# Closing a token mixer one head at a time, and a router constant from one matrix product

## The chip, the cores and the metric

The kernel runs on one core of one Trainium2 chip. The metric is the device time of one execution in microseconds (us); lower is better. The core has five engines that run their own queues in order and meet through semaphores: PE (TensorE, matrix products and transposes, with weight loads PEld), DVE (VectorE), ACT (ScalarE), POOL (GpSimd) and SP, which here only issues DMAs. A small share of the DMAs is issued from ACT's queue.

## The reference

A float32 model of two parts, 512 tokens by 1024 features. Two blocks (feed-forward, hybrid mixer, feed-forward) come first. Then a third block: a modulated token mixer (`token_mixer`) and an expert-choice mixture of experts (MoE), and a last norm. What the change touches is the end of the token mixer and the router:

```python
# token mixer, end: o is [1, 512, 4 heads, 128]
o = rmsnorm(o, dn_norm) * silu(gate)          # norm over 128 features of a head, one weight row for all heads
y = concatenate([o.reshape(B, L, 512), pooled], -1) @ w_out     # [512, 1024] @ [1024, 1024]
x = x + g1 * y
# mixture of experts
h = rmsnorm(x, norm2) * (1 + scale2) + shift2
aff = softmax(h @ w_router)                   # w_router: [1024, 16]
top_aff, top_idx = top_k(aff.T, 64)           # each expert takes 64 tokens
```

Each of 16 experts then applies a gated feed-forward (three 1024x1024 matrices) to its 64 tokens.

## The kernel before

Activations lie feature-major: `g.x[k]` is the k-th block of 128 features (partitions) by 512 tokens. A product in nearly full float32 precision is made of three passes (`mm3`, L69 to L71): weights and activations are split into a rounded part and a remainder (`whi`, `wlo`; `xh`, `xl`), one cast on ACT and one subtraction on DVE (`split`, L39 and L40). `load_w` loads a weight block into one of two `wraw` buffers and splits it into `whi`/`wlo`, of which there are three buffers each. The program is written in one order; a scheduler that runs when the program is built fixes the order of each engine's queue, and it may bring an instruction forward of where it is written.

The end of `token_mixer`. A recurrence over chunks (gated delta rule) writes `o_acc[c]` (in the profile `t_raw`), four tiles of 128 tokens by 512, four heads side by side. While it still runs, PE projects the gates (`gate`, in the profile `t_b`: ACT and DVE make their silu, L1403 to L1405) and begins the output product: `begun[t]`, t = 0 to 3, are four PSUM accumulators of 128 output features by 512 tokens, in which the pooled half of the input (blocks 4 to 7) has been summed. Then, when the recurrence is over:

- `oss` and `rsqrt` give `orn`, 1/rms for each token and head;
- for each of the four token tiles c, DVE scales the four heads by `orn` and by the norm weights `rows` (L1432, 16 instructions of 128x128), and POOL multiplies the tile by the gate (L1434, 4 of 128x512);
- PE transposes 128x128 blocks (L1438), four for a head k, into one PSUM bank, and `split` makes `yh[:, k]`, `yl[:, k]` of it (`xh`, `xl` in the profile). All four tiles c are needed for any head k.

`mixer_out` then finishes `begun[t]` with blocks 0 to 3 (12 matmuls of 512 columns for each t) from a weight block loaded by `load_w`, adds each to `g.x[t]` (`add`, L1452), and makes t = 4 to 7 with 24 matmuls each.

`mixer_out` is a generator: `moe` runs a step of its own for each block k that comes out: a square for the norm (ACT, POOL), `logits(k-1)` (L1557: 8 PE instructions, `r_ww` by x) and `turn_x(k-1)` (L1563: 4 transposes). The router weights `wr` (`r_w`) are loaded when `moe` begins, from ACT's queue (L1544), into a tile of the `moe` pool, whose memory overlaps that of the token mixer's tiles. `wrw` (`r_ww`) is `wr` times the norm weight (POOL, L1548). At k = 1 the constant `cst`, the shift times the router weights, is made by eight accumulated products of a broadcast column of `shift` with `wr` (L1576). After the last block come the router's softmax and the choice of 64 tokens for each expert (`route`), the gathering of the first two experts' tokens, and the experts, whose weights SP loads in chunks of 1 MB (L1534, L1539), 17 chunks ahead.

Of the kernel before, what the change touches and what calls it, by code (L numbers as in the profile page):

```python
# [11 lines left out]
F32 = mybir.dt.float32  # L12
# [9 lines left out]
NK = D // 128  # L22
# [14 lines left out]
def split(g, hi, lo, src):  # L37

    g.nc.scalar.copy(hi, src)  # L39
    g.nc.vector.tensor_sub(lo, src, f32(hi))  # L40
# [91 lines left out]
def stat_tiles(g):  # L132

    t = g.xpool.tile([128, 2 * S], F32, name="x")
    return t[:, :S], t[:, S:]
# [62 lines left out]
def bc(ap, shape):  # L198
    return ap.to_broadcast(shape)
# [52 lines left out]
def fm_proj(g, xh, xl, w, c0=0, ks=range(NK), k0=0, pump=None, p=None, last=True):  # L252


    first = p is None
    if first:
        p = g.ps_m.tile([128, 512], F32, name="mm")
    wh, wl = w
    cs = slice(c0, c0 + 128)
    mm3(g, p, lambda k: (wh[:, k - k0, cs], wl[:, k - k0, cs]), lambda k: (xh[:, k, :], xl[:, k, :]), ks, pump, first, last)  # L260
    return p
# [24 lines left out]
def sm(g):  # L286
    return g.ps_s.tile([128, 512], F32, name="sm")
# [963 lines left out]
def token_mixer(g, I):  # L1251
# [148 lines left out]
    for i, p in enumerate(ps):  # L1400
        z = gate[i // 2][:, i % 2, :]
        th = ring()
        nc.scalar.activation(th, p, AF.Tanh, scale=0.5)  # L1403
        nc.scalar.activation(z, p, AF.Copy, scale=0.5)
        nc.vector.scalar_tensor_tensor(z, th, 1.0, z, op0=OP.add, op1=OP.mult)  # L1405
        side.pump(4)
    pooled(3)

# [17 lines left out]
    nc.vector.scalar_tensor_tensor(oss, oss, 1.0 / 128, qe, op0=OP.mult, op1=OP.add)  # L1426
    orn = P.tile([128, NT, 4], F32, name="t_orn")
    rsqrt(g, orn, oss, P, "to")
    for c in range(NT):
        for h in range(4):  # L1430
            hs = slice(h * 128, (h + 1) * 128)
            nc.vector.scalar_tensor_tensor(o_acc[c][:, hs], o_acc[c][:, hs], orn[:, c, h:h + 1], rows,  # L1432
                                           op0=OP.mult, op1=OP.mult)
        nc.gpsimd.tensor_mul(o_acc[c], o_acc[c], gate[c // 2][:, c % 2, :])  # L1434
    for k in range(4):
        p = sm(g)
        for i in range(NT):
            nc.tensor.transpose(p[:, i * 128:(i + 1) * 128], o_acc[i][:, k * 128:(k + 1) * 128], g.ident)  # L1438
        split(g, yh[:, k, :], yl[:, k, :], p)
    return yh, yl, xd, begun  # L1440


def mixer_out(g, I, yh, yl, xd, begun):

    nc = g.nc
    order = (4, 5, 6, 7, 0, 1, 2, 3)
    g.xt = x_tiles(g)
    g.x = x_views(g.xt)
    for c in range(4):
        nc.sync.dma_start(g.xt[c].rearrange("p (k t) -> p k t", k=2), xd[2 * c:2 * c + 2].rearrange("k p t -> p k t"))  # L1450
    def add(t, p):
        nc.vector.scalar_tensor_tensor(g.x[t], p, g.mod[:, 16 + t:17 + t], g.x[t], op0=OP.mult, op1=OP.add)  # L1452

    w = load_w(g, I["w_out2"][0:512, 0:512], 512, 256)
    for t, p in enumerate(begun):
        add(t, fm_proj(g, yh, yl, w[t // 2], (t % 2) * 128, (0, 1, 2, 3), 0, p=p))
        yield t
    for c in range(2, 4):
        w = load_w(g, I["w_out2"][:, c * 256:(c + 1) * 256], 256)
        for m in range(2):  # L1460
            t = 2 * c + m
            add(t, fm_proj(g, yh, yl, w[m], 0, order))
            yield t
# [39 lines left out]
def moe(g, I, P, x_out, out):  # L1503
# [36 lines left out]
            loaded.append(raw)  # L1540


    wr = P.tile([128, NK, 16], F32, name="r_w")
    nc.scalar.dma_start(wr, I["w_router"].rearrange("(k p) e -> p k e", p=128))  # L1544
    wrw = P.tile([128, NK, 16], F32, name="r_ww")
    w = P.tile([128, NK], F32, name="nm_w")
    nc.vector.scalar_tensor_tensor(w, g.mod[:, 32:40], 1.0, v["norm2"], op0=OP.add, op1=OP.mult)
    nc.gpsimd.tensor_mul(wrw, wr, bc(w[:, :, None], [128, NK, 16]))  # L1548
    cst = P.tile([128, 16], F32, name="r_cst")
    acc, sq = stat_tiles(g)  # L1550
    pr = sm(g)

# [13 lines left out]
    for k in x_out:  # L1566
        nc.scalar.activation(sq if k else acc, g.x[k], AF.Square)
        if 0 < k < NK - 1:
            nc.gpsimd.tensor_add(acc, acc, sq)
        if k:  # L1570
            logits(k - 1)
            turn_x(k - 1)
        if k == 1:
            ps = sm(g)
            for j in range(NK):
                nc.tensor.matmul(ps[:, 0:16], bc(shift[:, j:j + 1], [128, 128]), wr[:, j, :], start=(j == 0),  # L1576
                                 stop=(j == NK - 1))
            nc.scalar.copy(cst, ps[:, 0:16])
        if k in (1, 3, 5):
            while len(loaded) < NR * (k + 1) // 6:  # L1580
                load()
# [308 lines left out]
def setup(g, I, P0):  # L1890
    nc = g.nc
    C = g.const
    _, at, _ = constants()
    cst = C.tile(list(I["cst"].shape), F32, name="cst")
    nc.scalar.dma_start(cst, I["cst"])
    for n, sl in at[0].items():
        setattr(g, n, cst[:, sl])

    r = g.small.tile([128, 284], F32R, name="cstr")
    for src, c0, c1 in ((g.ident, 0, 128), (g.mneg, 128, 256), (g.stk, 256, 284)):  # L1900
        nc.scalar.copy(r[:, c0:c1], src)
    g.eye_r, g.neg_r, g.stk8, g.stk4 = [r[:, a:b] for a, b in ((0, 128), (128, 256), (272, 280), (280, 284))]
    sel = g.small.tile([128, 16, 32], F32R, name="sel16")
    nc.scalar.copy(sel, bc(g.stk[:, 0:16][:, :, None], [128, 16, 32]))
    g.sel16 = sel.rearrange("p (t h) c -> p t (h c)", t=4)
    vecf = C.tile(list(I["vecf"].shape), F32, name="vecf")
    nc.scalar.dma_start(vecf, I["vecf"])
    g.vecr = I["vecr"]
    pf = [0]

    def tf(k):
        pf[0] += k
        return vecf[:, pf[0] - k:pf[0]]

    g.V = []
    for L in range(2):
        v = {}
        v["ffn1_norm"], v["mix_norm"], v["ffn2_norm"] = tf(8), tf(8), tf(8)
        v["conv_w"], v["conv_b"] = tf(32), tf(8)
        v["qk_w"] = tf(2)  # L1920
        v["snorm"] = tf(4)
        nc.vector.tensor_scalar(v["conv_w"], v["conv_w"], 0.5, None, op0=OP.mult)
        nc.vector.tensor_scalar(v["conv_b"], v["conv_b"], 0.5, None, op0=OP.mult)
        nc.vector.tensor_scalar(v["qk_w"][:, 0:1], v["qk_w"][:, 0:1], 32.0 ** -0.5, None, op0=OP.mult)
        g.V.append(v)
    v = dict(norm1=tf(8), norm2=tf(8), b_mod=tf(48), conv_w=tf(48), pool_scale=tf(4), c=tf(16), norm_f=tf(8))
    nc.vector.tensor_scalar(v["conv_w"], v["conv_w"], 0.5, None, op0=OP.mult)
    r2 = C.tile([128, 16], F32, name="row2")
    nc.scalar.dma_start(r2, bass.AP(tensor=I["vecr2"].tensor, offset=I["vecr2"].offset, ap=[[0, 128], [1, 16]]))
    v["dt_bias"], v["negA"] = r2[:, 0:8], r2[:, 8:16]  # L1930
    nc.scalar.activation(v["negA"], v["negA"], AF.Exp)
    nc.vector.tensor_scalar(v["negA"], v["negA"], -1.0, None, op0=OP.mult)
    g.V2 = v
    g.mod = C.tile([128, 48], F32, name="mod")
    g.modc = C.tile([128, 16], F32, name="modc")


def spread(g, I):
# [120 lines left out]
```

## Time and profile before

| | |
|---|---|
| median of 3 runs | 3046.94 us (3042.88 to 3048.18) |
| the profiled execution's own time | 3047.01 us |
| its span, first to last instruction | 3045.0 us |
| mean granted TensorE clock, as a share of 2.4 GHz | 0.971 |
| busy: PE, DVE, ACT, POOL | 95%, 54%, 30%, 10% of the span |
| DMA traffic | 471.51 MB, mean 155 GB/s |

Times in the profile are us from the span's start. A row of the timeline is a run of like instructions on one engine: start, duration, engine, source line, operation, output<-input, shape, count, and in brackets the idle time before it with what ended that. "x8" counts instructions as the profiler saw them; a 128x128 float32 product with 16 columns shows as two instructions. A matmul's duration includes the pipeline, so the rate is read from one start to the next.

### The profile page before, as it was taken

How to read it: one execution, taken by the hardware profiler on the slowest of the kernel's cores; microseconds unless marked ns; L12 is line 12 of the kernel's file. 1: busy time of each engine (PE TensorE's matmuls, PEld its weight loads, DVE VectorE, ACT ScalarE, POOL GpSimd, SP SyncE). 2: the span in 40 equal slices, each digit the busy share in tenths (PEclk: the TensorE clock that was granted, in tenths of full speed). 3: DMA queues.
4: the chain of work that ended last, by engine and by line, in shares of the span. 5: the costliest groups of instructions: out<-in, count | busy, mean ns of one | idle time of the engine just before them, and what ended most of it. 6: DMA issues, size and time to landing. Idle time of an engine off the chain costs nothing. (4 is left out here: it accounts for less than half of the span.)

```text
span 3045.0 us, 37744 instructions
## 1 busy us (share of the span) xinstructions
PE 2895.9 (95%) x15232; PEld 2220.4 (73%) x15232; DVE 1648.2 (54%) x2839; ACT 910.2 (30%) x1523; POOL 313.4 (10%) x260
## 2 busy tenths in 40 slices
PE   7999998999999999999899999999998877999998
PEld 6888886878888888888787788888787765444445
DVE  4445457665444599545586666554765643122213
ACT  3222335443222332223454433222342321010002
POOL 0001003110101102011130201201100010000000
PEclk9999999999999999999999999999999988999998
DMA  4433343122332358333421333222323435999996
GB/s 144 128 97 97 102 143 120 53 87 83 97 97 93 115 195 299 100 93 132 142 63 59 103 101 111 86 76 90 114 71 90 116 150 201 397 423 424 423 423 253
DMA packets 293107, 471.51 MB, mean 155 GB/s; under 512 B 45215, under 2 KB 237727, under 8 KB 269508
## 3 DMA queue, kind: packets, MB, share of 16 engines
q1 hardware_dynamic: 290216, 466.28, 43.5%
q10 hardware_dynamic: 2716, 2.82, 0.3%
q8 instruction: 120, 1.97, 0.3%
q14 instruction: 55, 0.45, 0.0%
HBM read 449.38 MB, written 19.67 MB: 154 GB/s over the span
## 5 line engine op out<-in xcount | busy, mean ns | idle before, releaser
L69 PE MATMUL mm<-xh,whi 128*128 128x512 f32 x1952 | 780.0, 401 | 15.6 <-ACT xh L146 8.4
L70 PE MATMUL mm<-xl,whi 128*128 128x512 f32 x1952 | 774.2, 397 | 0.0
L71 PE MATMUL mm<-xh,wlo 128*128 128x512 f32 x1952 | 770.6, 395 | 1.1 <-DVE wlo L40 1.1
L39 ACT CAST whi<-wraw 128x1024 fp32r<-128x1024 f32 (+3 forms) x390 | 391.7, 1005 | 1123.3 <-PE mm L70 795.0
L40 DVE TENSOR_TENSOR wlo<-wraw,whi 128x1024 fp32r<-128x1024 f32 (+3 forms) x390 | 516.6, 1325 | 106.5 <-ACT whi L39 99.2
L69 PEld LDWEIGHTS mm<-xh,whi 128*128 128x128 f32 x1952 | 372.9, 191 | 99.5 <-ACT xh L146 9.3
L71 PEld LDWEIGHTS mm<-xh,wlo 128*128 128x128 f32 x1952 | 372.0, 191 | 79.4 <-DVE wlo L40 1.9
L70 PEld LDWEIGHTS mm<-xl,whi 128*128 128x128 f32 x1952 | 372.5, 191 | 76.2 <-DVE xl L147 1.2
L69 PE MATMUL mm<-hh,whi 128*128 128x512 f32 x704 | 279.3, 397 | 0.0
L70 PE MATMUL mm<-hl,whi 128*128 128x512 f32 x704 | 278.6, 396 | 0.0
L71 PE MATMUL mm<-hh,wlo 128*128 128x512 f32 x704 | 278.3, 395 | 0.0
L192 POOL TENSOR_TENSOR x<-x,dt 128x512 f32<-128x512 f32 x72 | 112.9, 1568 | 873.2 <-DVE dt L191 778.6
L172 DVE TENSOR_TENSOR gs<-mm,rb 128x512 f32<-128x512 f32 x88 | 60.8, 691 | 202.9 <-PE mm L71 198.5
L177 DVE TENSOR_TENSOR gs<-gs,mm 128x512 f32<-128x512 f32 x88 | 60.4, 687 | 197.1 <-PE mm L71 197.0
L191 DVE SCALAR_TENSOR_TENSOR dt<-mm,rb 128x512 f32<-128x512 f32 x104 | 71.8, 690 | 166.9 <-PE mm L71 166.9
L71 PEld LDWEIGHTS mm<-hh,wlo 128*128 128x128 f32 x704 | 132.1, 188 | 32.1
L70 PEld LDWEIGHTS mm<-hl,whi 128*128 128x128 f32 x704 | 132.2, 188 | 31.7 <-DVE hl L40 0.3
L69 PEld LDWEIGHTS mm<-hh,whi 128*128 128x128 f32 x704 | 132.1, 188 | 31.6
L1651 PE MATMUL mm<-e_raw,e_x 128*64 128x512 f32 x504 | 118.9, 598 | 0.0
L238 PE MATMUL mm<-whi,xh 128*128 128x512 f32 (+2 forms) x288 | 103.3, 359 | 0.0
L240 PE MATMUL mm<-whi,xl 128*128 128x512 f32 (+2 forms) x288 | 100.0, 348 | 0.0
L239 PE MATMUL mm<-wlo,xh 128*128 128x512 f32 (+2 forms) x288 | 99.7, 346 | 0.0
(649 smaller groups left out, 3555.4 us busy)
## 6 DMA issues: line engine op xcount, KB each, us to landing
wraw<-ffn_gate SPq DMA_DIRECT2D x44, 1024.0 KB, 5.4
wraw<-ffn_up SPq DMA_DIRECT2D x44, 1024.0 KB, 5.3
wraw<-w_in SPq DMA_DIRECT2D x38, 1024.0 KB, 5.3
e_raw<-e_gate SPq DMA_DIRECT2D x36, 1024.0 KB, 12.4
e_raw<-e_up SPq DMA_DIRECT2D x27, 1024.0 KB, 13.2
e_raw<-e_down SPq DMA_DIRECT2D x25, 1024.0 KB, 13.2
wraw<-ffn_down SPq DMA_DIRECT2D x24, 1024.0 KB, 5.1
mw<-w_mod SPq DMA_DIRECT2D x24, 1024.0 KB, 5.1
```

The lines of the kernel that those rows point to most:

```text
L39: g.nc.scalar.copy(hi, src)
L40: g.nc.vector.tensor_sub(lo, src, f32(hi))
L69: g.nc.tensor.matmul(out, lh, rh, start=first and i == 0, stop=False, skip_group_check=not (first and last))
L70: g.nc.tensor.matmul(out, lh, rl, start=False, stop=False, skip_group_check=not (first and last))
L71: g.nc.tensor.matmul(out, ll, rh, start=False, stop=last and i == n - 1, skip_group_check=not (first and last))
L172: nc.vector.tensor_mul(gs, pg, rb)
L191: nc.vector.scalar_tensor_tensor(t, pd, 0.25, rb, op0=OP.mult, op1=OP.mult)
L192: (nc.vector if c0 + nch == sum(groups) else nc.gpsimd).tensor_add(g.x[2 * c + m], g.x[2 * c + m], t)
L238: nc.tensor.matmul(o, xh[:, kk, ts], wh[:, k, :], start=(kk == 0), stop=False)
L239: nc.tensor.matmul(o, xh[:, kk, ts], wl[:, k, :], start=False, stop=False)
L240: nc.tensor.matmul(o, xl[:, kk, ts], wh[:, k, :], start=False, stop=(kk == NK - 1))
L1651: nc.tensor.matmul(ps[h][pj[j], :], lhs(k, j), raw[j][:, h * 512:(h + 1) * 512], start=(k == 0), stop=(k == NK - 1), skip_group_check=True)
```

## The change

Four edits. (1) The norm weights are multiplied into the gates as each gate tile is made (POOL, new line under L1405, 4 instructions of 128x512), and POOL's multiplication of `o_acc` by the gate goes away: DVE's 16 instructions now multiply by `orn` and by the gate. (2) The 16 are ordered by head: four for head k, its transposes and split, then the 12 matmuls that head k contributes to the four `begun` tiles; the weights for these are loaded in `token_mixer` instead of in `mixer_out`, which only adds the finished tiles. (3) The router weights go into a tile of the constants' pool and are loaded in `setup`, at the beginning of the kernel. (4) The constant: POOL multiplies the router weights by the shift into `ws` (128 x 16 x 8), DVE sums over 8, and one product with a matrix of ones sums over the partitions, in place of eight products.

```diff
@@ token_mixer
         nc.vector.scalar_tensor_tensor(z, th, 1.0, z, op0=OP.add, op1=OP.mult)
+        nc.gpsimd.tensor_mul(hv(z), hv(z), bc(rows[:, None, :], [128, 4, 128]))
         side.pump(4)
...
     rsqrt(g, orn, oss, P, "to")
-    for c in range(NT):
-        for h in range(4):
-            hs = slice(h * 128, (h + 1) * 128)
-            nc.vector.scalar_tensor_tensor(o_acc[c][:, hs], o_acc[c][:, hs], orn[:, c, h:h + 1], rows,
-                                           op0=OP.mult, op1=OP.mult)
-        nc.gpsimd.tensor_mul(o_acc[c], o_acc[c], gate[c // 2][:, c % 2, :])
+    w = load_w(g, I["w_out2"][0:512, 0:512], 512, 256)
     for k in range(4):
+        hs = slice(k * 128, (k + 1) * 128)
+        for c in range(NT):
+            nc.vector.scalar_tensor_tensor(o_acc[c][:, hs], o_acc[c][:, hs], orn[:, c, k:k + 1],
+                                           gate[c // 2][:, c % 2, hs], op0=OP.mult, op1=OP.mult)
         p = sm(g)
         for i in range(NT):
-            nc.tensor.transpose(p[:, i * 128:(i + 1) * 128], o_acc[i][:, k * 128:(k + 1) * 128], g.ident)
+            nc.tensor.transpose(p[:, i * 128:(i + 1) * 128], o_acc[i][:, hs], g.ident)
         split(g, yh[:, k, :], yl[:, k, :], p)
+        for t in range(4):
+            fm_proj(g, yh, yl, w[t // 2], (t % 2) * 128, (k,), 0, p=begun[t], last=k == 3)
     return yh, yl, xd, begun
@@ mixer_out
-    w = load_w(g, I["w_out2"][0:512, 0:512], 512, 256)
     for t, p in enumerate(begun):
-        add(t, fm_proj(g, yh, yl, w[t // 2], (t % 2) * 128, (0, 1, 2, 3), 0, p=p))
+        add(t, p)
         yield t
@@ moe
-    wr = P.tile([128, NK, 16], F32, name="r_w")
-    nc.scalar.dma_start(wr, I["w_router"].rearrange("(k p) e -> p k e", p=128))
+    wr = g.wr
...
     cst = P.tile([128, 16], F32, name="r_cst")
+    ws = P.tile([128, 16, NK], F32, name="r_ws")
+    nc.gpsimd.tensor_mul(ws, wr.rearrange("p k e -> p e k"), bc(shift[:, None, :], [128, 16, NK]))
+    nc.vector.reduce_sum(cst, ws, axis=AX.X)
...
         if k == 1:
             ps = sm(g)
-            for j in range(NK):
-                nc.tensor.matmul(ps[:, 0:16], bc(shift[:, j:j + 1], [128, 128]), wr[:, j, :], start=(j == 0),
-                                 stop=(j == NK - 1))
+            nc.tensor.matmul(ps[:, 0:16], g.ones, cst, start=True, stop=True)
             nc.scalar.copy(cst, ps[:, 0:16])
@@ setup
+    g.wr = C.tile([128, NK, 16], F32, name="r_w")
+    nc.scalar.dma_start(g.wr, I["w_router"].rearrange("(k p) e -> p k e", p=128))
```

## Rows read from the trace of the kernel before

**Rows 1.** Chain that ended last, 2469 to 2570: start us, us, what.
```profile
2469.98 15.26 DMA r_w<-w_router
...
2567.56 13.02 PE mm L1651 x58
```

**Rows 2.** Busy time by stretch: PE, PEld, DVE, ACT, POOL, then clock, DMA, GB/s.
```profile
2600.00:2700.00 100.00, 99.92 (x518) 45.28 (x516) 18.39 (x33) 9.21 (x17) 0.00 (x0) 1.00 1.01 421
```

**Rows 3.** Timeline, all engines, 2469 to 2531.
```profile
2469.76 2.08 PE L69 MATMUL mm<-xh,whi 128*128 128x512 f32 x4
2469.80 5.30 SPq L1534 DMA_DIRECT2D e_raw<-e_gate  x8
2469.91 2.48 DVE L40 TENSOR_TENSOR xl<-sm,xh 128x512 fp32r<-128x512 f32 x4
...
2471.63 0.63 PE L70 MATMUL mm<-xl,whi 128*128 128x512 f32 x1
...
2473.77 0.63 PE L69 MATMUL mm<-xh,whi 128*128 128x512 f32 x1
...
2476.56 0.39 PE L69 MATMUL mm<-xh,whi 128*128 128x512 f32 x1
...
2477.69 0.39 PE L71 MATMUL mm<-xh,wlo 128*128 128x512 f32 x1
...
2485.36 0.40 POOL L1548 TENSOR_TENSOR r_ww<-r_w,nm_w 128x128 f32<-128x128 f32 x1 [16.80 <-DMA r_w<-w_router]
...
2485.82 1.89 PE L1557 MATMUL sm<-r_ww,x 128*128 128x16 f32 x8 [7.74 <-POOL r_ww L1548]
...
2488.43 3.43 PE L1576 MATMUL sm<-r_w,mod 128*128 128x16 f32 x16
...
2495.75 0.96 PE L1557 MATMUL sm<-r_ww,x 128*128 128x16 f32 x8
...
2499.55 0.96 PE L1557 MATMUL sm<-r_ww,x 128*128 128x16 f32 x8
...
2530.07 0.95 PE L106 MATMUL sm<-cst,x 128*128 128x2 f32 x8
```

**Rows 4.** Timeline, all engines, 2459 to 2470.
```profile
2459.80 7.35 DVE L1432 SCALAR_TENSOR_TENSOR t_raw<-t_raw,t_orn,t_rows 128x128 f32<-128x128 f32 x16
2461.11 1.47 POOL L1434 TENSOR_TENSOR t_raw<-t_raw,t_b 128x512 f32<-128x512 f32 x1 [20.32 <-DVE t_raw L1432]
...
2468.61 1.11 PE L1438 MATMUL sm<-cst,t_raw 128*128 128x128 f32 x4 [0.97 <-POOL t_raw L1434]
2469.12 1.08 ACT L39 CAST xh<-sm 128x512 fp32r<-128x512 f32 x2 [12.88 <-PE sm L1438]
```

**Rows 5.** Busy time by stretch, 2455 to 2531, columns as in rows 2.
```profile
2455.40:2462.60 7.20, 0.00 (x0) 0.00 (x0) 6.79 (x22) 0.84 (x1) 1.47 (x1) 0.86 0.00 0
...
2469.70:2474.20 4.50, 4.46 (x12) 3.51 (x12) 2.56 (x5) 1.48 (x4) 0.00 (x0) 0.50 0.68 234
...
2485.80:2491.60 5.80, 5.78 (x28) 5.78 (x28) 0.00 (x0) 1.12 (x2) 1.26 (x1) 0.50 1.01 424
...
2495.50:2531.00 35.50, 35.50 (x209) 31.01 (x207) 6.95 (x8) 9.40 (x15) 6.45 (x5) 1.00 0.34 120
```

**Rows 6.** Timeline, DVE and POOL, 2437 to 2441.
```profile
2437.30 1.12 DVE L1148 SCALAR_TENSOR_TENSOR t_raw<-sm,t_gex,t_raw 128x128 f32<-128x128 f32 x4
...
2440.18 0.61 POOL L1119 COPY t_u<-x 64x512 f32<-64x512 f32 x1 [25.83 <-DVE x L1108]
```

**Rows 7.** Timeline, ACT: a cast of the weights for heads 2 and 3.
```profile
2420.48 1.05 ACT L39 CAST whi<-wraw 128x1024 fp32r<-128x1024 f32 x1 [3.69 <-PE mm L70]
```

**Rows 8.** Instructions on tile t_raw: duration ns min/median/max, first and last start.
```profile
L1432 DVE SCALAR_TENSOR_TENSOR t_raw<-t_raw,t_orn,t_rows x16: 339/347/1368, 2459.8 to 2466.8; 128x128 f32<-128x128 f32 x16
```

**Rows 9.** Timeline, the kernel's first microseconds.
```profile
5.42 0.62 ACT L1901 CAST cstr<-cst 128x128 fp32r<-128x128 f32 x3 [1.30 <-DMA cst<-cst]
```

**Rows 10.** DMA queue of ACT, 2469 to 2487: packets, MB, share.
```profile
q10 hardware_dynamic: 1040, 0.07, 3.9%
```

## The prediction

> **What bounds the kernel now.** I began at the end of the chain of waits and went back to the stretch that the change touches. The last stage, the experts, starts with its first product at 2567.56 [rows 1]. The table of stretches shows PE busy 99.92% there and the DMA engines full as well [rows 2]; the listed waits of PE name no DMA. Whichever of the two is the limit, the stage is a fixed length of work that begins when the first product begins, so the end moves one for one with 2567.56. What comes before it (the choice of tokens, the first gather, 36.5 us from the end of the router's products to 2567.56) is a chain that the change leaves alone. So the question is how much earlier PE finishes the router's products, which it does at 2530.07 + 0.95 = 2531.0 [rows 3].
>
> The timeline from 2459 shows what sets that. `orn` is ready at 2459.80; DVE's 16 scalings and POOL's four products run in turn, and since every head needs all four token tiles, PE gets its last four transposes only at 2468.61 [rows 4]. The 48 matmuls that finish `begun` start at 2469.76 and go through 26 of the 48 until 2477.69; then PE's queue holds `logits(0)`, which needs `r_ww`, which needs the router weights: their DMA, issued at 2469.98 once the token mixer's memory is free, lands after 15.3 us [rows 1], and PE stands still for 7.74 us [rows 3]. It comes back at half clock: the granted clock is 0.50 from 2485.8 to 2491.6, and in that time PE also works off the 16 instructions of the constant [rows 3, 5]. From 2495.5 on it is at full clock and 35.50 of 35.50 us busy [rows 5].
>
> Two rates. At the low clock (1.2 GHz) five matmul steps take 2473.77 - 2471.63 = 2.14, so 0.428 us each; at 2.4 GHz 2477.69 - 2476.56 = 1.13, so 0.226 [rows 3].
>
> **The change part by part.**
>
> *The heads.* Before, without the stall, the 22 matmuls left after 2477.69 would end at 2477.92 + 22 x 0.226 = 2482.9. After the change: POOL's four products are gone. The first four scalings end at about 2461.1 (POOL could start at 2461.11 behind four of them) [rows 4]. Transposes of head 0 take 1.11 at the low clock, to 2462.2; head 1's follow, to 2463.3. ACT's cast (0.54, half of 1.08) [rows 4] and DVE's remainder (0.62, a quarter of 2.48) [rows 3] have `yh`, `yl` of head 0 at 2463.4. From there PE has 12 matmuls for each head. DVE needs 16 x 0.28 (four in 1.12 [rows 6]) + 4 x 0.62 = 7.0, until 2466.8, well ahead of the 36 matmuls of the other heads. PE stands idle before this just as before, and I take the clock as after 2469.70, where dense work ran 4.5 us at 0.50 before it rose [rows 5]: 10.5 matmuls by 2467.9, 37.5 x 0.226 = 8.5 after, and two more sets of transposes at 0.55: end 2477.5. Gain 5.4. Bounds: full clock throughout 7.6; half clock throughout (48 x 0.428 + 2.2 from 2463.4, 2486.1) a loss of 3.2.
>
> *The stall.* With the router weights on the chip since setup, `r_ww` needs only DVE's `nm_w`, whose memory comes free with the last head's transposes, and 0.40 of POOL [rows 3]: ready by about 2470, before x[0] at 2477. The whole gap from 2477.92 to 2485.82 goes: 7.9. Bounds 0 (another wait takes its place) to 7.9. SP's first loads wait for the same transposes (2469.80 [rows 3]) and move by about 1 us, not more.
>
> *The constant and the clock after the stall.* From 2485.82 to 2495.75, 9.93 us, PE did `logits(0)`, `turn_x(0)`, the constant and 11 matmuls; from 2495.75 to 2499.55, 3.80 us, the same without the constant, at full clock [rows 3]. The new single product is two instructions of 0.12 (an eighth of 0.96). Gain 9.93 - 3.80 - 0.24 = 5.9. If PE comes to it at half clock, only the 16 instructions go, about 3.2. The new POOL product and DVE sum for `ws` are of 128x128 elements: 0.40 each, by POOL's product of that size [rows 3], hidden behind the heads' matmuls; uncovered 0.8.
>
> *The load moved forward* is worth nothing: the cast of the second half of that weight block already ran at 2420.48, forty microseconds before its use [rows 7]. The number and order of `whi`/`wlo` buffers are the same.
>
> *Norm weights into the gates.* Four POOL products of 128x512, 1.26 to 1.47 each [rows 4], now run where L1405 makes the gates, while the recurrence is alive, the last two shortly before 2440. POOL has little else there, but `t_u` at 2440.18 [rows 6] stands in POOL's queue behind the last two, and the recurrence waits for it. A second price is what POOL does to DVE. The 16 scalings, both operands in SBUF, took 7.35 beside four POOL products [rows 4], against 16 x 0.28 = 4.5 by a scaling with one operand in PSUM [rows 6]; one took 1368 ns where the median is 347 [rows 8]. That is 2.9 for four, 0.7 for each. Below nothing is excluded, as POOL gives no work back to the recurrence; the ceiling is the full length of all four, 5.9. DVE's scalings of the recurrence read PSUM for one operand [rows 6], so I take half of 2.9, 1.5.
>
> By the Trainium skill (SBUF — State Buffer, "Who interferes with whom") a DVE instruction with two SBUF inputs and a GpSimd instruction that reads SBUF exclude each other for a whole instruction. The one scaling of 1368 ns agrees; the other fifteen near 347 do not show it each time. The sum goes by the rows; by the rule at its worst it would be 3033.2 in place of 3029.5, the second rival.
>
> *The load in setup.* ACT's issue falls into the time before 5.42 in which ACT waits 1.30 for the constants anyway [rows 9]. In 2469 to 2487 that queue's 1040 packets, nearly all of them this load, took 3.9% of the DMA engines [rows 10], 0.7 us of all sixteen. Bounds 0 to 0.7; I take 0.2, since the first weights wait in any case behind ACT's squares.
>
> Sum: 5.4 + 7.9 + 5.9 - 1.5 - 0.2 = 17.5. Against the profiled execution's 3047.0, which is the median of the runs (3046.9) within 0.1: 3029.5.
>
> **The rivals.**
>
> 1. *The heads run one after another.* If the queue order holds the matmuls of head k ahead of the transposes of head k+1, PE waits in each head for cast and remainder: per head 0.55 + 0.54 + 0.62 + 12 x 0.226 = 4.4, after a first head that ends at 2468.5 (12 x 0.428 from 2463.4). Three more end at 2481.7; the gain of the heads falls from 5.4 to 1.2: 3033.7. For it: the order is fixed when the program is built, and it has put a waiting `logits(0)` ahead of ready matmuls once already [rows 3]. Against: four transposes were taken tile by tile as they became ready, ahead of the order written [rows 4].
>
> 2. *POOL holds DVE for the whole of each product* in the recurrence: 4 x 1.3 = 5.2 in place of 1.5, 3033.2. For it the 1368 ns; against it, the mix of operands above. This is what the rule of the SBUF page would do here.
>
> 3. *Another wait in place of the router weights.* x[0] to x[3] now come within some 3 us, and behind them stand ACT's squares and copies, POOL's sums (1.26 each, with one buffer `sq`) and the casts of the next weights. If PE's queue has one of these in front, up to 7.9 + 5.9 comes back: 3029.5 + 13.8 = 3043.3, no measurable change. Against: PE has t = 4 (24 x 0.226 = 5.4 us) needing nothing but the first accumulator back, and four `logits` to work on.
>
> 4. *The weights' DMA sets the end.* The first 17 chunks, 17.8 MB at 421 GB/s [rows 2], need 42 us from 2469.80, to 2512; the first product would come at 2550. There are 38 us of slack, so the stage moves whole; if it did not, the time stays near 3046.
>
> 5. *Slower: PE stays at 1.2 GHz.* The heads' matmuls are now cut by transposes and splits. If the clock stayed low from 2461 through the output product and the router, the heads end at 2486.1, then 96 matmuls at 0.428 (41.1), eight `logits` with transposes at 2.61 (2485.82 to 2488.43 [rows 3], 20.9) and the statistics at twice 1.9 (3.8), with the constant 0.5: PE ends at 2552.4, 21.4 later than now, 3070 with the costs above. It decides from the point where the low clock has eaten 17.5: 35 us at 1.2 GHz. Against it: the same mixture of work ran 35.5 us at 1.00 [rows 5]. The Trainium skill (TensorE: Matmul & The Clock Gate, "HAM oscillation") describes kernels whose clock falls again at every wait for data; what this trace shows of it is the fall to 0.50 around each idle stretch [rows 5].
>
> **How the numbers follow.** Forecast 0.60 (3025 to 3034 as its own range); heads in turn 0.12; POOL's hold 0.08; another wait 0.10, half of it above and half below what can be measured; DMA 0.03; low clock 0.05; a larger gain, heads at full clock and no costs (3025.6 and below), 0.02. A measurement tells about 0.2% (6 us) from no change. Faster: 0.60 + 0.12 + 0.08 + 0.02 + 0.05 = 0.87; same 0.05 + 0.03 = 0.08; slower 0.05. The range: 3029.5 less 2.2 for the clock and 1.7 for the costs gives 3025.6, and a few us below it for what the scheduler may reorder, 3022; upward the first two rivals together (3037.4) and part of the third, 3040.
>
> **What would show it.** No POOL product between the 16 scalings and the transposes; matmuls on `begun` from about 2463; no wait of PE for `r_ww`; PE at the end of the router's statistics near 2512, the first expert product near 2550, and the length from there to the end as before. Wrong would be: a recurrence that ends later than now by more than 2 us, gaps of PE between heads, a new wait among `logits`, or a granted clock of 0.5 after 2470.

## The result: 20.5 us less, and where the profile shows them

The changed kernel takes 3027.01 us (median of 4 runs, 3022.43 to 3028.21) against 3047.56 for the kernel before on the same chip (4 runs, 3042.88 to 3048.35): ratio 0.9932, 95% interval 0.992 to 0.9943. Its profiled execution took 3025.99, its span is 3024.2, 20.8 less than before. The forecast was 3029.5.

The start of the experts, in the chain that ended last (start, us, what), answers to [rows 1]. As there, it is the long group of 58 products; six of the first expert's products stand a few us ahead of it:

```profile
2547.35 13.02 PE mm L1652 x58
```

It moved by 20.2 us. The timeline of the changed kernel, from the first scaling to the last product of the router, answers to [rows 3, 4]:

```profile
2457.83 2.45 DVE L1434 SCALAR_TENSOR_TENSOR t_raw<-t_raw,t_orn,t_b 128x128 f32<-128x128 f32 x9
...
2458.33 1.96 PE L1438 MATMUL sm<-cst,t_raw 128*128 128x128 f32 x7 [5.06 <-DVE t_raw L1434]
...
2460.17 1.65 PE L69 MATMUL mm<-xh,whi 128*128 128x512 f32 x3
...
2460.80 1.92 DVE L1434 SCALAR_TENSOR_TENSOR t_raw<-t_raw,t_orn,t_b 128x128 f32<-128x128 f32 x7
...
2465.00 0.93 PE L1438 MATMUL sm<-cst,t_raw 128*128 128x128 f32 x7
...
2471.53 0.38 PE L1438 MATMUL sm<-cst,t_raw 128*128 128x128 f32 x2
...
2471.97 4.10 SPq L1535 DMA_DIRECT2D e_raw<-e_gate  x8
...
2472.58 1.21 PE L69 MATMUL mm<-xh,whi 128*128 128x512 f32 x4 [0.68 <-ACT xh L39]
2472.59 0.40 POOL L1548 TENSOR_TENSOR r_ww<-r_w,nm_w 128x128 f32<-128x128 f32 x1
...
2475.56 0.96 PE L1560 MATMUL sm<-r_ww,x 128*128 128x16 f32 x8
...
2476.84 0.29 PE L1578 MATMUL sm<-r_cst,cst 128*128 128x16 f32 x2
...
2506.74 0.95 PE L106 MATMUL sm<-cst,x 128*128 128x2 f32 x8
...
2509.00 1.70 PE L106 MATMUL sm<-cst,x 128*128 128x2 f32 x8
```

Three things are to be seen. The 16 scalings take 2.45 + 1.92 and not 7.35, and PE's matmuls on `begun` start 2.3 us after the first of them. `r_ww` is ready at 2472.99 and `logits(0)` follows at 2475.56 with no idle time in brackets: the wait of 7.74 is gone. The constant is 0.29. All of PE's longest waits from 2440 to 2540 (in total, times, longest) are these; none names `r_ww`, and the first and third lie in the choice of tokens:

```profile
PE sm L1499 <- DVE e_full L1495: 15.3, 1, 15.3
PE sm L1438 <- DVE t_raw L1434: 5.1, 1, 5.1
PE sm L1482 <- DVE r_aff L1479: 4.6, 1, 4.6
PE sm L1614 <- DVE e_ohr L1607: 1.9, 1, 1.9
PE mm L69 <- ACT xh L39: 0.7, 1, 0.7
```

The granted clock (third column from the right; the table of stretches, against [rows 5, 2]):

```profile
2457.00:2458.00 1.00, 0.00 (x0) 0.00 (x0) 0.78 (x5) 0.00 (x0) 0.00 (x0) 0.81 0.00 0
2458.00:2464.00 6.00, 5.67 (x16) 4.32 (x17) 4.71 (x17) 0.58 (x1) 0.00 (x0) 0.50 0.00 0
...
2465.00:2508.00 43.00, 42.30 (x240) 36.17 (x239) 12.55 (x16) 13.05 (x22) 9.10 (x8) 1.00 0.61 252
...
2509.00:2511.00 2.00, 1.70 (x9) 1.61 (x8) 0.23 (x2) 0.58 (x1) 0.00 (x0) 0.50 1.02 430
2600.00:2700.00 100.00, 99.91 (x506) 45.20 (x502) 24.56 (x45) 9.36 (x17) 0.00 (x0) 1.00 1.01 424
```

One spell at half clock after PE's idle time, none behind a stall, and a new one from 2508.6, which makes the last group 1.70 long where its twin before it took 0.95. The experts run as before, PE and DMA engines full.

Since one execution differs from the next, each kernel was profiled a second time (experiments 9 and 10). The marks, in us from the span's start:

| | before | before again | changed | changed again |
|---|---|---|---|---|
| first scaling | 2459.80 | 2459.60 | 2457.83 | 2459.83 |
| `logits(0)` | 2485.82 | 2485.53 | 2475.56 | 2476.42 |
| rsqrt of the second norm (DVE) | 2531.06 | 2530.83 | 2510.74 | 2510.77 |
| first expert product | 2567.56 | 2567.37 | 2547.35 | 2547.15 |
| span | 3045.0 | 3045.0 | 3024.2 | 3024.2 |

From the first scaling to the rsqrt it is 71.26 and 71.23 before, 52.91 and 50.94 after (52.95 in a third profile, experiment 11): 18.3 to 20.3 us of the 20.8 lie in this stretch.

### The profile page after: what moved, and what is told of

Its sections match the earlier page's. It is cut to its first block, busy times and chain, and to the rows that moved or that the text cites. A ratio compares the mean times of both kernels' runs of the same rounds, so it can differ in the third digit from the quotient of the medians.

```text
span 3024.2 us, 37711 instructions
## 1 busy us (share of the span) xinstructions
PE 2886.7 (95%) x15218; PEld 2212.8 (73%) x15218; DVE 1640.1 (54%) x2840; ACT 907.8 (30%) x1523; POOL 321.7 (11%) x261
## 4 chain that ended last, share of the span: by engine, by line
PE 82%; DVE 8%; issue 4%; ACT 2%; POOL 2%; DMA 2%; SPq 0%; POOLq 0%; ACTq 0%; DVEq 0%
PE mm L69 19%; PE mm L70 18%; PE mm L71 18%; PE mm L1652 11%; PE sm L1614 2%; PE sm L1097 1%; PE sm L1142 1%; PE sm L1670 1%; DVE wlo L40 1%; PE mm L240 1%; PE mm L238 1%; PE mm L239 1%; PE sm L106 1%; POOL x L155 1%; PE sm L660 1%
## 5 line engine op out<-in xcount | busy, mean ns | idle before, releaser
L40 DVE TENSOR_TENSOR wlo<-wraw,whi 128x1024 fp32r<-128x1024 f32 (+3 forms) x390 | 509.5, 1307 | 105.7 <-ACT whi L39 98.3
L192 POOL TENSOR_TENSOR x<-x,dt 128x512 f32<-128x512 f32 x72 | 120.5, 1674 | 866.5 <-DVE dt L191 772.8
```

Of the source, the lines that this page charges most:

```text
L192: (nc.vector if c0 + nch == sum(groups) else nc.gpsimd).tensor_add(g.x[2 * c + m], g.x[2 * c + m], t)
```

## The experiments

**1 and 2. Each part alone.** Experiment 1 has the heads' part (edits 1 and 2) and the router as before; experiment 2 the router's part (edits 3 and 4) and the heads as before.

```diff
# experiment 1, against the changed kernel
-    wr = g.wr
+    wr = P.tile([128, NK, 16], F32, name="r_w")
+    nc.scalar.dma_start(wr, I["w_router"].rearrange("(k p) e -> p k e", p=128))
...
-            nc.tensor.matmul(ps[:, 0:16], g.ones, cst, start=True, stop=True)
+            for j in range(NK):
+                nc.tensor.matmul(ps[:, 0:16], bc(shift[:, j:j + 1], [128, 128]), wr[:, j, :], start=(j == 0),
+                                 stop=(j == NK - 1))
```

Expected of experiment 1:

> Heads part alone (norm weights in the gates, end of the mixer by head); router weights and constant as before. Theory (one queue, one late DMA): the heads' matmuls end about 18 us after orn, as in the changed kernel, but logits(0) still stands next in PE's queue and the router weights still land 15.3 us after the mixer's memory is free. That is later than before, since the last head's transposes now stand behind the matmuls of three heads: PE idle about 12 us, then half clock and the constant. PE ends the router's products 70 to 72 us after orn (before: 71.2), so the time is that of the kernel before within 3 us. Rival (the parts add up): 5.4 us faster, 3042, router's products ended 65.8 us after orn.

Measured: 3046.28 (11 runs, 3043.26 to 3049.12), ratio 1.0001 (0.9992 to 1.001). Its timeline:

```profile
2471.93 0.41 ACTq L1545 DMA_DIRECT2D r_w<-w_router  x1
...
2489.77 1.89 PE L1558 MATMUL sm<-r_ww,x 128*128 128x16 f32 x8 [14.45 <-POOL r_ww L1549]
...
2492.38 3.43 PE L1577 MATMUL sm<-r_w,mod 128*128 128x16 f32 x16
```

The heads finish as early as in the changed kernel, and PE then waits 14.45 us for `r_ww` where it waited 7.74 [rows 3]. The load is issued 14.2 us after the first scaling (2457.78), 4 us later than before, since its memory comes free with the last head's transposes, and lands behind SP's loads after 17 us. What the heads give, this wait takes, and more: from the first scaling to the rsqrt it is 75.63 us (2533.41), where 71.26 was the kernel before and 70 to 72 expected. About 0.6 of it is a fall of the clock ahead of the last group of products (1.54 in place of 0.95). In the median time the two kernels cannot be told apart.

Expected of experiment 2:

> Router part alone (weights loaded in setup, constant by one product); end of the mixer as before. Theory: the stall of 7.9 and the 5.9 after it go whatever the heads do: 13.8 less 0.7 for the setup load, about 3034; PE ends the router's products 57.4 us after orn. Rival 1 (the load of the weights is not what PE waited for, the next thing in line is): under 3 us faster. Rival 2 (parts add up with the heads' 5.4): the same 13.8, so only together with the run of the heads alone does it tell.

```diff
# experiment 2, against the kernel before
-    wr = P.tile([128, NK, 16], F32, name="r_w")
-    nc.scalar.dma_start(wr, I["w_router"].rearrange("(k p) e -> p k e", p=128))
+    wr = g.wr
...
+    nc.vector.reduce_sum(cst, ws, axis=AX.X)
...
+            nc.tensor.matmul(ps[:, 0:16], g.ones, cst, start=True, stop=True)
```

Measured: 3031.64 (5 runs, 3030.22 to 3032.17), ratio 0.9955 (0.9942 to 0.9967). In its timeline the scalings beside POOL are long again, and nothing waits for `r_ww`:

```profile
2457.46 7.36 DVE L1432 SCALAR_TENSOR_TENSOR t_raw<-t_raw,t_orn,t_rows 128x128 f32<-128x128 f32 x16
...
2475.47 0.96 PE L1559 MATMUL sm<-r_ww,x 128*128 128x16 f32 x8
...
2514.82 0.16 DVE L109 TENSOR_SCALAR rs_ms<-sm 128x4 f32<-128x4 f32 x1 [3.50 <-PE sm L106]
```

The stretch from first scaling to rsqrt is 57.36, so 13.9 less than before: the 7.9 + 5.9 of the prediction. That `r_ww` comes in time is what does it (rival 1 had under 3 us). From 2475 to 2495, where the kernel before stood still and then ran at half clock, PE is busy 20.00 of 20.00 us at a granted clock of 1.00. With the heads' part on top the stretch is 50.94 to 52.95. So the heads are worth 4.4 to 6.4 us behind the router's part, and without it they gave no time that can be measured; the parts do not add up from single trials.

**3. The constant alone.** The changed kernel with the constant by eight products:

```diff
-    nc.gpsimd.tensor_mul(ws, wr.rearrange("p k e -> p e k"), bc(shift[:, None, :], [128, 16, NK]))
-    nc.vector.reduce_sum(cst, ws, axis=AX.X)
...
-            nc.tensor.matmul(ps[:, 0:16], g.ones, cst, start=True, stop=True)
+            for j in range(NK):
+                nc.tensor.matmul(ps[:, 0:16], bc(shift[:, j:j + 1], [128, 128]), wr[:, j, :], start=(j == 0),
+                                 stop=(j == NK - 1))
```

> The changed kernel with the constant by eight accumulated products as before, at k = 1, weights still from setup. Theory: at full clock 16 instructions of 0.12 against one product seen as two (0.29 in all): 1.6 to 1.7 us slower than the changed kernel in the stretch from the last head's matmul to the end of the router's products, 3028 to 3029. Rival (its price is what it was before, at half clock): 3.0 us or more. Rival (PE has slack there): no change.

Measured: 3026.77 (4 runs, 3022.57 to 3027.4), ratio 0.9936 (0.9923 to 0.995), in time not to be told from the changed kernel. The timeline gives its price:

```profile
2476.39 0.96 PE L1557 MATMUL sm<-r_ww,x 128*128 128x16 f32 x8
...
2477.67 1.86 PE L1576 MATMUL sm<-r_w,mod 128*128 128x16 f32 x16
...
2479.38 1.04 PE L1557 MATMUL sm<-r_ww,x 128*128 128x16 f32 x8
```

From `logits(0)` to the start of the seventh of the eight `logits` (2507.79) it is 31.40 us, with one product (2505.46) 29.90: 1.5 us. So of the 5.9 that the prediction put on "the constant and the clock", these 1.5 belong to the constant once the stall is gone; the other 4.4 were the half clock behind the stall, and went with the stall. The split depends on the order: at half clock the eight products took 3.28 us (2488.43 to 2491.71 in the kernel before), at full clock 1.71.

**4. POOL's price in the recurrence.** The changed kernel with three more POOL products behind each gate product, times ones: 12 more, which change no value.

```diff
         nc.gpsimd.tensor_mul(hv(z), hv(z), bc(rows[:, None, :], [128, 4, 128]))
+        for _ in range(3):
+            nc.gpsimd.tensor_mul(hv(z), hv(z), bc(g.ones[:, None, :], [128, 4, 128]))
```

> The changed kernel with three more POOL products of each gate tile with ones, so that twelve products of 128x512 are added inside the recurrence; the values stay the same. Theory: POOL's price is only what stands behind it in its queue. In the built queue the second copy of t_u stands behind all the extra products of the last two gates, which begin 4.3 us before it: eight products of about 1.27 end at about 10.2 us after the third gate, so the copy, and with it the recurrence, comes about 6 us later: 3033; orn late by about 6 us; DVE's instructions slowed by under 1 us. Rival (a POOL product holds DVE for its whole length): 12 times 1.3 more, 15 us, spread over the whole stretch, 3042. Rival (POOL has room for all of it): no change.

Measured: 3031.9 (4 runs, 3029.41 to 3033.08), ratio 0.9955 (0.9941 to 0.9969), 4.9 us over the changed kernel and 5.1 over experiment 3, which ran on the same chip and whose runs do not overlap with these. The size is near the expected 6, but the cause is for the most part another. The timeline shows two prices:

```profile
2400.63 1.15 DVE L1071 TENSOR_TENSOR t_scr<-dl_X,dl_D 64x16 f32<-64x16 f32 x1
...
2403.41 1.12 DVE L1071 TENSOR_TENSOR t_scr<-dl_X,dl_D 64x36 f32<-64x36 f32 x1
...
2408.43 1.98 PE L1097 MATMUL sm<-x 64*64 64x64 f32 x32 [4.18 <-DVE x L1108]
...
2424.21 2.32 DVE L40 TENSOR_TENSOR wlo<-wraw,whi 128x1024 fp32r<-128x1024 f32 x1 [1.92 <-ACT whi L39]
...
2443.09 5.22 POOL L1408 TENSOR_TENSOR t_b<-t_b,cst 128x512 f32<-128x512 f32 x4
...
2448.37 0.61 POOL L1119 COPY t_u<-x 64x512 f32<-64x512 f32 x1
...
2449.03 1.38 PE L1142 MATMUL sm<-t_scr,t_u 128*128 128x128 f32 x10 [1.18 <-POOL t_u L1119]
```

The larger price is DVE's. On DVE runs a chain of small products and sums (L1071, L1072: it builds a triangular inverse row by row in `dl_X`), for which the recurrence waits; each product has both inputs in SBUF. The four POOL products of the first gate tile hold one of these each: 1.18, 1.15, 1.15 and 1.12, where the changed kernel has one of 1.18 and then 0.18, 0.20 and 0.21. PE then waits 4.18 for DVE, in the changed kernel 1.36, and goes on at a granted clock of 0.50 until 2412.9, in the changed kernel at 1.00. Let the common mark be the start of the product of 64x4 in this chain, the last one ahead of the first gate product (2398.86 here, 2400.09 in the changed kernel). From it to the scalings at L1148 ahead of `t_u` it is 43.76 us (2442.62) against 38.84: 4.9 are lost before `t_u`.

The smaller price is POOL's queue: `t_u` stands behind the products, and PE waits 1.18 for it. From the common mark to the first scaling (2462.98) it is 64.12, against 57.74 and 57.94 in two profiles of the changed kernel: 6.2 to 6.4 in all. One more DVE instruction with both inputs in SBUF, the remainder of a weight block, takes 2.32 beside POOL and 1.22 in the changed kernel; the delay is 4.8 ahead of it and 4.9 behind it, so it costs little. So the expectation that DVE would lose under 1 us was wrong. The rival's mechanism is there, for four of the twelve added products and not for all, which is why its 15 us did not come.

**5 to 8. What the new order still costs.** Experiment 5 puts all heads' transposes and splits ahead of the matmuls; 6 moves the load of the router weights from the setup to the start of the token mixer; 7 fills PE's idle time ahead of the first transposes with 32 products of the identity with itself, whose results are overwritten; 8 is all three.

```diff
# 5
         split(g, yh[:, k, :], yl[:, k, :], p)
+    for k in range(4):
         for t in range(4):
             fm_proj(g, yh, yl, w[t // 2], (t % 2) * 128, (k,), 0, p=begun[t], last=k == 3)
# 6, in token_mixer in place of setup
+    nc.scalar.dma_start(g.wr, I["w_router"].rearrange("(k p) e -> p k e", p=128))
# 7
     side.drain()
+    p = sm(g)
+    for i in range(32):
+        nc.tensor.matmul(p[:, i % 4 * 128:(i % 4 + 1) * 128], g.ident, g.ident, start=True, stop=True)
```

> The changed kernel, with the transposes and splits of all four heads written ahead of the matmuls that finish the begun sums. In the changed kernel the last head's two transposes stand behind the products of heads 0 to 2, and TensorE waits twice for a split (0.26 and 0.68 us). If these waits are what the order a head at a time costs, they go: the stretch from the first scaling to the DVE rsqrt of the second norm, 52.9 us in the changed kernel, becomes 51.9 to 52.4, and the time is that of the changed kernel less at most 1 us (3026), which the rounds cannot tell from it. Rival: with all transposes ahead, the first product starts later (the one at 2460.17 us would wait for more scalings at half clock), and the stretch grows by 1 to 5 us, towards the 5.4 us that the heads' part was worth.

> The changed kernel, with the load of the router weights issued from ACT at the start of the token mixer and not in the setup. If the 0.7 us by which everything ran late from the start of the changed kernel is this one issue ahead of the vectors in ACT's queue, the first weights' cast is at 18.2 to 18.4 us again (19.1 in the changed kernel), and the wait for the scaled router weights stays away: time 3026, at most 0.7 us under the changed kernel, not to be told by the rounds. Rival: the 1040 small packets, now beside the token mixer's own loads, hold one of its weights or vectors up, and the time is 1 to 4 us over the changed kernel.

> The changed kernel, with 32 products of the identity with itself (into a PSUM tile that the first head's transposes then overwrite) in the 5.1 us in which TensorE has nothing between the recurrence and the first transposes. They compute nothing that is used. If the granted clock's fall to half from 2456 to 2464 us comes from that idle gap, it stays at full speed: the first head's 12 matmuls take 2.8 us and not 4.8, and the stretch from the first scaling to the rsqrt of the second norm (52.9 us) becomes 50.5 to 51.4. Time 3024 to 3026. Rival 1: VectorE's and ACT's splits set the pace here anyway; TensorE only waits longer for xh, and the stretch stays within 0.5 us of 52.9. Rival 2: the PSUM tile is let go too late, the 32 products run into the transposes, and the stretch grows by 1 to 3 us.

> The three together: transposes of all heads first, router weights loaded at the start of the token mixer, and the identity's products in the gap. If the three shares are there and add up (0.7 at the start, 0.5 to 1 for the waits, 1.5 to 2.4 for the clock), the time is 3022 to 3024.5 and the ratio to the kernel before 0.9917 to 0.9928. Rival: the pace between the first scaling and the logits is set by VectorE's scalings and the splits, so that the shares overlap: 3025 to 3026.5, as the changed kernel.

Measured: 3023.58 (3022.23 to 3027.66), 3025.54 (3025.42 to 3025.77), 3023.57 (3022.27 to 3025.35) in 4 runs each, 3022.28 (3019.75 to 3023.11) in 5; ratios 0.9932 (0.9918 to 0.9945), 0.9936 (0.9923 to 0.995), 0.993 (0.9916 to 0.9944) and 0.9924 (0.9911 to 0.9938). These overlap each other and the changed kernel's. From the first scaling to the rsqrt it is 50.90, 52.92, 50.34 and 50.00 us, against 50.94 to 52.95 in three profiles of the changed kernel.

Experiment 5 does what it was to do. Its last two transposes come before the matmuls of the later heads, and `logits(0)` comes 16.55 us after the first scaling (2457.38) instead of 17.73, with half clock up to 2464.3 or 2464.4 in both:

```profile
2465.28 0.38 PE L1438 MATMUL sm<-cst,t_raw 128*128 128x128 f32 x2
...
2473.93 0.96 PE L1561 MATMUL sm<-r_ww,x 128*128 128x16 f32 x8
```

Experiment 6 missed its number: the first weights' cast is at 18.83, not 18.2 to 18.4. With the load in the setup it lies at 18.64 to 19.23 in eight executions, with the load at the start of the token mixer at 18.60 to 18.83 in the three executions of experiments 6, 8 and 12, and at 18.20 and 18.30 before. But experiment 1, which loads the router weights as late as the kernel before, has 18.77. So it is not shown that the load causes any of that lateness.

Experiment 7: in these stretches PE is busy with the filler and then with the heads, and the clock holds:

```profile
2458.00:2460.00 2.00, 2.00 (x20) 2.00 (x20) 1.85 (x8) 0.00 (x0) 0.00 (x0) 1.00 0.03 8
...
2462.00:2464.00 2.00, 2.00 (x8) 1.53 (x9) 1.81 (x5) 0.43 (x1) 0.00 (x0) 1.00 0.00 0
```

The filler ran on until 2460.7, into the time of the transposes (as its second rival had it), and still `logits(0)` comes 15.98 us after the first scaling (2458.32). So the half clock of that stretch follows the idle gap, and costs the changed kernel at least 0.6 to 1.8 us. By the Trainium skill (TensorE: Matmul & The Clock Gate, "HAM oscillation") the clock falls over waits in which PE has nothing to do; this stretch agrees, 1.00 with the gap filled (so also in experiments 8 and 12) and 0.50 without.

**9 and 10. Each kernel once more.**

> The kernel before, unchanged, for a second profiled execution. In the one shown first its first scaling began at 2459.80 us, 2.0 us later than in the changed kernel (2457.83), and in all other kernels of this study but the one with more POOL work it began between 2456.65 and 2458.69 us. If these 2 us are one execution against another, the first scaling begins here between 2456.5 and 2460 us, and the stretch from it to the rsqrt of the second norm is 71.3 us within 1 us, whatever its start. Rival: the change itself gave them (by the gate products that POOL no longer has), and the first scaling begins at 2459.5 to 2460.1 us again.

> The changed kernel, unchanged, for a second profiled execution. The first scaling begins between 2456.5 and 2459 us. The stretch from it to the rsqrt of the second norm is 52.9 us if the granted clock falls before the last four products of the norm's sum again (0.76 and 1.70 us for the last groups of lines 1566 and 106), and 52.1 us if that fall was one execution's.

Before: 3047.07; first scaling at 2459.60, the stretch 71.23. This start lies in both expected ranges, so experiment 9 does not decide. Changed: 3025.99, as in its first profile to the hundredth, with the marks of the table above; its first scaling, at 2459.83, lies outside the expected 2456.5 to 2459. From its timeline and table of stretches:

```profile
2509.78 0.95 PE L106 MATMUL sm<-cst,x 128*128 128x2 f32 x8
```

```profile
2460.00:2461.00 1.00, 0.67 (x3) 0.47 (x3) 1.00 (x5) 0.00 (x0) 0.00 (x0) 0.79 0.00 0
2461.00:2464.00 3.00, 3.00 (x9) 2.23 (x9) 3.00 (x11) 0.59 (x1) 0.00 (x0) 0.50 0.00 0
```

The 2.0 us earlier start of the first changed profile is thus not always there, and 1.9 of the 2.0 lie ahead of the gates' edit: the common mark of experiment 4 is at 2400.09 in the first changed profile, 2401.89 in the second, 2401.97 and 2401.64 in the kernel before. I count it as the execution's, not the change's. That is not fully shown: the other ten profiles with any part of the change (experiment 4 apart) start the scalings at 2456.65 to 2458.69, ahead of both profiles of the kernel before. Behind the start the low clock lasts 3.4 us here and 6.8 there, so that `logits(0)` comes 16.59 and not 17.73 after the first scaling; and the clock does not fall ahead of the last group (0.95, not 1.70).

**11 and 12. The combination beside the changed kernel.**

> The changed kernel once more, timed on the same chip as the combination below: 3024 to 3028.

> The combination of experiments 5 to 7 once more, beside the changed kernel on one chip. From the stretches (first scaling to the second norm's rsqrt 49.95 us, against 50.94 and 52.9 in two executions of the changed kernel) and the start (first weights' cast 18.6 against 18.64 and 19.13): 1 to 3.4 us less than the changed kernel. Rival: the difference seen so far (3022.3 against 3027.0) is one chip's run against another's, and the two medians lie within 1 us.

Measured on one chip, 5 runs each: changed 3026.08 (3022.78 to 3026.99), combination 3025.26 (3023.62 to 3026.54); ratios 0.9936 (0.9923 to 0.995) and 0.9935 (0.9922 to 0.9947). The rival holds: 0.8 us, no difference that can be measured. (Alone, experiment 8 had come within its expected time and ratio.) In this execution the combination's `logits(0)` came 15.63 us after its first scaling, early as in experiment 8 (15.65), but the clock fell ahead of the last group (1.71) and took 1.4 us of it back.

## Why the prediction was right, and where its sizes were off

*What bounds the kernel*: right. The experts' stage moved whole; from its first product to the end it is 477.4 before and 476.9 after, and the 0.6 stays unexplained. DMA did not take over (rival 4), although SP's first loads left 2.2 us later than before and not the 1 us of the prediction, since the last head's transposes end only at 2471.91.

*The stall*, 7.9: right. `r_ww` was ready at 2472.99, 3 us later than predicted, and still 2.6 us ahead of its use; in experiment 2, too, nothing waits for it. No other wait took its place (rival 3).

*The constant and the clock*, 5.9: right in sum. `logits(0)` to rsqrt shrank from 45.24 to 34.35 in the second changed profile; 22 matmuls of 0.226 that now run earlier are 5.0 of these 10.9, so 5.9 are left. In the first changed profile the late fall of the clock takes back 0.8. The name of the term misleads: 1.5 was the constant, 4.4 the clock after the stall (experiment 3).

*The heads*, 5.4: `logits(0)` was to come 17.7 us after the first scaling and came 17.73 and 16.59 after it, so 5.4 to 6.5. The first figure hits by luck, by two errors that cancel. The first product came 2.3 us after the first scaling, not 3.6, since transposes start after single scalings and three products with `xh` go ahead of the remainder; and PE then waited twice for a cast (0.26 and 0.68), because the queue holds seven transposes behind the matmuls of head 0 and the last two behind those of heads 0 to 2. That is a small piece of rival 1, and the gaps between heads that the prediction named as a sign of being wrong; experiment 5 takes them away.

*Norm weights into the gates*, a loss of 1.5: the step that went wrong, though the number was not far off. The error is in the reading of [rows 8]. I took the maximum of 1368 for one scaling out of 16 and the other fifteen for 347. A minimum, a median and a maximum do not say how many are near the maximum. The timeline of the kernel before, cut to short windows at three of POOL's products, has pairs of scalings:

```profile
2461.12 1.61 DVE L1432 SCALAR_TENSOR_TENSOR t_raw<-t_raw,t_orn,t_rows 128x128 f32<-128x128 f32 x2
```

```profile
2462.92 1.63 DVE L1432 SCALAR_TENSOR_TENSOR t_raw<-t_raw,t_orn,t_rows 128x128 f32<-128x128 f32 x2
```

```profile
2465.00 1.63 DVE L1432 SCALAR_TENSOR_TENSOR t_raw<-t_raw,t_orn,t_rows 128x128 f32<-128x128 f32 x2
```

Two scalings take 0.61 together without POOL (0.26 from start to start, 0.35 the last). So three scalings were held for 1.0 us each, one for each POOL product that met them, and 3 x 1.0 is the whole difference between 7.35 and 4.37. The Trainium skill (SBUF — State Buffer, "Who interferes with whom") says that a DVE instruction with two SBUF inputs and a GpSimd instruction that reads SBUF shut each other out for a whole instruction; here the trace agrees each time, and the prediction's sentence that fifteen scalings speak against it was wrong. What kept rival 2 from coming true in full is the other half of the same section, that a DVE instruction with at most one SBUF input, outside its two-port modes, is not held. In the recurrence the scalings read PSUM for one input, and eight of them take 2.15 beside a gate product and 2.14 without. But two instructions with both inputs in SBUF did meet a gate product, one for 1.0 us in the chain of experiment 4 (1.18 instead of 0.16) and one for 0.4 (1.05 instead of 0.68). The changed kernel:

```profile
2400.32 1.29 POOL L1406 TENSOR_TENSOR t_b<-t_b,t_rows 128x512 f32<-128x512 f32 x1 [16.67 <-DVE t_scr L1071]
...
2400.45 1.18 DVE L1071 TENSOR_TENSOR t_scr<-dl_X,dl_D 64x9 f32<-64x9 f32 x1
...
2422.80 0.30 PE L1097 MATMUL sm<-x 64*64 64x64 f32 x2 [2.99 <-DMA x<-ds]
...
2433.89 1.26 POOL L1406 TENSOR_TENSOR t_b<-t_b,t_rows 128x512 f32<-128x512 f32 x1 [16.02 <-DVE t_b L1405]
2434.65 1.05 DVE L1405 SCALAR_TENSOR_TENSOR t_b<-t_scr,t_b 128x512 f32<-128x512 f32 x1
...
2438.21 0.61 POOL L1119 COPY t_u<-x 64x512 f32<-64x512 f32 x1 [1.15 <-issue]
```

The kernel before:

```profile
2402.34 0.16 DVE L1071 TENSOR_TENSOR t_scr<-dl_X,dl_D 64x9 f32<-64x9 f32 x1
...
2423.49 0.44 PE L1097 MATMUL sm<-x 64*64 64x64 f32 x2 [2.82 <-DMA x<-ds]
```

The 1.0 lies on the path. From the common mark (2400.09 and 2401.97) to the PE products that need the chain's result, by way of a DMA, it is 22.71 us here and 21.52 before. That is so in all profiles: 22.5 to 22.9 in ten with the edit (experiment 4 left out), 21.5 to 21.7 in three without. Yet from the mark to the first scaling it is 57.74, 57.94 and 56.21 in three profiles of the changed kernel, and 57.83 and 57.96 before. The loss is made good just behind, where PE comes out of this wait (granted clock third from the right; before, then changed):

```profile
2418.00:2431.00 13.00, 10.18 (x100) 8.71 (x100) 4.25 (x10) 2.62 (x4) 0.00 (x0) 0.74 0.52 130
```

```profile
2416.10:2429.10 13.00, 10.01 (x113) 8.65 (x113) 5.29 (x13) 2.70 (x4) 1.31 (x1) 0.87 0.55 147
```

PE ran at half clock for 6.8 us there in the three profiles without the edit, for 3.4 in six with it, and not at all in four with it; in those four, the third profile of the changed kernel among them, the first scaling comes 56.0 to 56.2 us after the mark. Why the spell is shorter is not shown. So the price was there, 1.0 to 1.2 on the path, by one held product and not by half a share of each, and it did not reach the first scaling because of a clock spell that the prediction did not have in its sum. `t_u`, the wait that it did name, came no later from the second gate tile's products: it starts at 2438.21 and 2440.19 in the two changed profiles, 2440.18 and 2440.00 before, and the first scaling follows 19.6 us later in all four. The better sum would have asked, for each DVE instruction near the gates, where its inputs lie and what waits for it.

*The load moved forward*, nothing: right; no wait for these weights appears. (The block in [rows 7] holds the weights of the output blocks t = 2 and 3, not of heads.) *The load in the setup*, 0.2: its reason failed. ACT's issue did not fit into the wait of 1.30: ACT's first cast came at 7.37 and 6.88 in place of 5.42 and 5.31. What it cost is open: the first weights' cast was 0.3 to 0.9 us later in the two changed profiles, but 0.5 to 0.6 later in experiment 1 too, without this load.

*The low clock* (rival 5): right that it would end, since dense work follows. It lasted 3.4 and 6.8 us in the two profiles. In one of them it came back ahead of the last products, which is one of the prediction's signs of being wrong (0.5 after 2470), at a price of 0.8.

In sum 5.4 to 6.5, 7.9 and 5.9 less 0 to 0.8 are 18.4 to 20.3. The profiled executions gained 21.0 where the prediction had 17.5. Of the 3.5 between, the gates' 1.5 and the load's 0.2 that did not show are 1.7, the experts 0.6; the rest is 2.0 of the early start less 0.8 of the late clock in the first profile, and the heads' 1.1 in the second. The median of the runs is 2.5 us below the forecast, inside its range.

## What to carry to other kernels

A wait hides what is ahead of it: work made shorter before a late DMA is worth nothing until the DMA is early too, so trial edits on one path together and singly. A stall on PE has a second price, the half clock behind it (4.4 us here behind 7.7), which disappears with the stall. Before costing POOL work beside DVE, list DVE's neighbours by the place of their inputs and by what waits for them, and count the long instructions, as a maximum does not say how many there are. A mark that comes no later does not show that nothing was lost: measure from a common mark ahead of the change, and look at what came between.

## What the runs showed that was not expected

The same program's clock spells differ from one execution to the next. After the same idle gap of 5.06 us half clock lasted 3.4 or 6.8 us. Ahead of the last products of the router the clock fell in 5 of the 11 profiles of kernels with the heads' part, among them two of the changed kernel's three and one of the combination's two, and in none of the three without it. PE had then been without a listed wait for 35 us or more; what brings this fall was not found. Such spells move a mark by 1 to 2 us while the whole time stays within its spread: two executions of the changed kernel with first scalings 2 us apart ended at the same 3025.99.

The load of the router weights, nearly all of the 1040 packets of [rows 10], lands after 2.3 us when issued at 18.7 us, 6.3 to 7.4 in the setup, 15.3 and 17 beside the experts' loads. So its size says little of when it lands; what else is under way seems to say more.
